# Attention output kept in SBUF, projections moved into the attention, a written order and an f32 tile before the experts

## The chip, the core and the metric

The kernel runs on one core of one Trainium2 chip. The metric is the device time of one execution in microseconds. The core has five engines that run side by side and meet through semaphores: TensorE (PE, matmuls; PEld are its weight loads), VectorE (DVE), ScalarE (ACT), GpSimd (POOL) and SyncE (SP, which here only issues DMAs). Sixteen DMA engines serve the queues that SP and POOL fill.

## The reference

One layer over 1024 tokens of width 1024, all in float32. Cut to what matters:

```python
def reference(x, w_in, ..., w_out, ln1_g, ln1_b, w_route_group, ..., w_gate, w_up, w_down, ln2_g, ln2_b):
    proj = einsum(x, w_in)                     # q, k, v, indexer, z, xbc, dt
    att = dsa_attention(q, k, v, iq, ik, iw)   # 8 heads of 64, each query keeps its 256 best keys
    ssd = ssd_mixer(z, xbc, dt, ...)           # chunked state-space scan, 8 chunks of 128
    mixed = concatenate([att, ssd]) @ w_out
    x = layer_norm(ALPHA * x + mixed, ln1_g, ln1_b)
    # 16 experts in 4 groups: the best group, its 2 best experts
    for e in range(16):
        hid = silu(x @ w_gate[e]) * (x @ w_up[e])          # width 256
        y = y + gates[..., e:e + 1] * (hid @ w_down[e])
    return layer_norm(ALPHA * x + y, ln2_g, ln2_b)
```

## The kernel before

Tokens are worked in eight blocks of 128. Matrices go through PE in float32r, and where precision matters an operand is split into a high part (a copy by ACT, `hi_act`) and a rest (a subtraction by DVE, `lo_dve`), so that one product takes three matmuls. The order of the instructions on each engine is chosen when the program is built, by a planner that simulates the engines and takes the first ready instruction by program order; at run time each engine and each DMA queue executes its list strictly in order. `tc.manual_schedule` makes the order as written binding for the engines that it names; `tc.issue_after` puts an instruction behind another on its engine. Buffers come from pools; a tile of a tag with n buffers waits until the oldest user of its buffer is done.

The stages: input projections, indexer and the choice of keys (0 to about 250 us), the state-space part (to about 370 us), attention over the blocks in `ORDER` = 7, 6, ..., 0 (from about 300 us), the step to the experts, the expert tiles, and the last normalisation.

**Attention and projection.** Python generators emit small steps, and `weave` mixes several of them by weights. `attn(b, nxt)` ends with `to_mix`, which transposes the block's output and writes its two parts (L808 to L810), and stores them to a DRAM tensor `td`. `mix(b)` loads them back (`ai`, L990), with the state-space part (`si`) and the block of x (`xb`), and makes 48 matmuls of 128x512 with the split w_out (`woh`, `wol`, L1006), adds x (L1010), takes the statistics (POOL raises the variance to the power -0.5, L554), transposes for the router (L1019), makes the router's 8 f32 matmuls (L1024; each is two instructions), writes the normalised rows to `hd` and `yd` (L1036, L1037), and, outside the last two blocks, goes on with `route`. `route(b)` ranks the experts, counts with two small matmuls (L1076, L1077), forms the places in the expert lists (`idx`, L1087), and scatters token and gate into `lst` by two indirect DMAs of POOL (L1094). `MIXAT` says with which attention block the projections of which earlier one are woven: before, block number i (in the order) with the projection of i - 2, so that those of the last two blocks, 1 and 0, follow the attention.

**Step to the experts** (L1161 to L1218). `pick` chooses the four fullest experts early (`EE`); `fill_up` declares the first 128 places of the two fullest as full, so that their first tiles can be gathered before the last two blocks are routed. Weights arrive in pieces of 1 MB in five raw buffers `er` (`fetch`, L862 to L865): two for gate and up, one for down, per expert. `split_expert` splits each piece in four (L880) into slots, the first in `eb`, the others in the memory of `woh` and `wol`; a piece whose split is done lets the piece five later be fetched. `expert_tile` gathers 128 rows by the list (`gather`, L888), transposes them (L898), multiplies by gate and up (24 matmuls, L909), applies silu, transposes, multiplies by down (12 matmuls, L934), scales by the gate and adds the rows to `yd` in DRAM by an indirect DMA (L941). The block from L1199 on emits, in written turns, the rest of block 0's `mix` (m0), the routes of blocks 1 and 0 (r1, r0), the two early tiles (t0, t1), the splits of their experts (sp0, sp1) and `order`, which sorts the experts by their counts; the planner is still free in it, since `MAN` is empty. One further tile (`NG0` = 1) is gathered there; its ids are loaded by SP (L1214).

**Expert tiles.** 22 further tiles follow in the order of `PLAN`, each with its gather three tiles ahead (`AHEAD`, L1244), and then `finish`.

Of the kernel before, what the change touches and what calls it, by code (L numbers as in the profile page):

```python
# [12 lines left out]
F32 = mybir.dt.float32  # L13
# [41 lines left out]
MIXAT = {i: (i - 2,) for i in range(2, NB)}  # L55
# [9 lines left out]
NG0 = 1  # L65
HFT = 1
PPT = 'po'
FO = 3
# [38 lines left out]
def f(ap):  # L107
    return ap.bitcast(F32)


def body(ctx, tc, I, out, dbg):
# [80 lines left out]
    td = dram.tile([S, D], F32, name="td")  # L192
# [608 lines left out]
    def attn(b, nxt):  # L801
# [90 lines left out]
    def expert_tile(W, ids, xg, al):  # L892
        th = al([P, KC, P], F32R, "th")
        tl = al([P, KC, P], F32R, "tl")
        for j in range(2):
# [5 lines left out]
            lo_dve(tl[:, js, :], pt, th[:, js, :])  # L901
# [13 lines left out]
        V.tensor_tensor(sg, ag[:, 256:], sg, op=OP.mult)  # L915
        ph2 = psum([P, 2, P], "ph2", "po")
        for k in range(2):
            T.transpose(ph2[:, k, :], sg[:, k * P:(k + 1) * P], ident)  # L918
        hh = al([P, 2, P], F32R, "hh")
        hl = al([P, 2, P], F32R, "hl")  # L920
        hi_act(hh, ph2)
        lo_dve(hl, ph2, hh)
# [3 lines left out]
        hi, lo = W["d"]  # L926
        for hf in range(2):
# [3 lines left out]
            for k in range(2):  # L931
                for j in range(3):
                    l, r = ((hh, hi), (hl, hi), (hh, lo))[j]
                    T.matmul(ad_, l[:, k, :], r[:, k, fs], start=i == 0, stop=i == 5)  # L934
                    i += 1
# [9 lines left out]
    with ExitStack() as ph:  # L945
# [41 lines left out]
        def mix_load(b):  # L987
            ao, so = (wc.tile([P, KC, P], F32R, name=nm, bufs=2) for nm in ("ai", "si"))
            for t, src in ((ao, td), (so, sd)):
                SY.dma_start(f(t), src[b * P:(b + 1) * P, :].rearrange("p (k t) -> p k t", t=P))  # L990
            xb = wc.tile([P, D], F32, name="xb", tag="xb", bufs=4)
            SY.dma_start(xb, x_d[b * P:(b + 1) * P, :])
            return ao, so, xb

        def mix(b, loaded=None):
            while (b, 0) not in done:
                yield
            ao, so, xb = loaded or mix_load(b)
# [37 lines left out]
            SY.dma_start(hd[b * P:(b + 1) * P, :], xb)  # L1036
# [64 lines left out]
        def order():  # L1101
            sq = [P, NE, NE]
            key, w1, cnt, rank = (wc.tile([P, NE], F32, name=nm) for nm in ("key", "w1", "cnt", "rank"))
            cc = wc.tile([P, 2, NE, NE], F32, name="cc", tag="rT", bufs=2)
# [19 lines left out]
            V.tensor_copy(ovi, ov)  # L1124

# [22 lines left out]

# [217 lines left out]
```

## Time and profile before

| | us |
|---|---|
| median of 3 runs | 908.57 (906.67 to 912.49) |
| the profiled execution | 908.86 |
| its span, first to last instruction | 907.2 |

A line of a timeline gives the start in us from the start of the span, the duration in us (for several instructions, from the first start to the last end), the engine, the line of the kernel, the operation, the tiles (written <- read) and the count; in brackets stands how long the engine sat idle before it and what released it. A matmul's duration contains its way through the array, so the distance from start to start tells more than the duration. PEclk is the granted TensorE clock as a share of 2.4 GHz; 0.50 is 1.2 GHz.

### The profile page before, as it was taken

What the parts mean: (1) busy time and instruction counts of PE and PEld (TensorE: products, weight loads), DVE (VectorE), ACT (ScalarE), POOL (GpSimd) and SP (SyncE); (2) the same over time, 40 slices, a digit from 0 to 9 for tenths busy, and PEclk for the clock granted to TensorE, in tenths of its full rate; (3) what the DMA queues carried; (4) which work ended last, traced back from release to release, by engine and by line L of the source; (5) the groups of instructions that cost most, each with busy time, mean ns of one, the idle gap of its engine ahead of it and who ended that gap; (6) DMA issues with size and microseconds to landing.
All of it is one profiled execution on the core that took longest, in us unless ns stands there. A gap on an engine that the chain in (4) does not pass through costs nothing. (4 is left out here: it accounts for less than half of the span.)

```text
span 907.2 us, 12832 instructions
## 1 busy us (share of the span) xinstructions
PE 789.6 (87%) x4084; PEld 649.5 (72%) x4085; DVE 663.2 (73%) x1644; ACT 507.2 (56%) x1074; POOL 222.1 (24%) x203
## 2 busy tenths in 40 slices
PE   6999789999997999899999999987998989969800
PEld 4898568887775678788898877765886767758600
DVE  3678978879576999768866865865775858739348
ACT  3467777882455876655434422634765657638323
POOL 2211000001387373250010111132122223132225
PEclk9999899999997999999999998997999999979955
DMA  8303112311434325873333335978899989989374
GB/s 232 106 24 93 37 69 94 117 47 68 132 128 157 99 70 208 257 266 117 105 105 118 140 117 182 337 247 253 237 278 270 316 260 283 324 255 260 60 225 183
DMA packets 90742, 155.95 MB, mean 172 GB/s; under 512 B 14613, under 2 KB 60837, under 8 KB 90666
## 3 DMA queue, kind: packets, MB, share of 16 engines
q1 hardware_dynamic: 83242, 129.87, 42.7%
q0 software_dynamic: 7424, 25.19, 11.7%
q8 instruction: 33, 0.54, 0.3%
q14 instruction: 43, 0.35, 0.1%
HBM read 109.78 MB, written 45.25 MB: 171 GB/s over the span
## 5 line engine op out<-in xcount | busy, mean ns | idle before, releaser
L232 PE MATMUL acc<-whl,xh 128*128 128x512 f32 (+1 forms) x384 | 121.6, 391 | 2.1 <-ACT whl L124 0.7
L232 PEld LDWEIGHTS acc<-whl,xh 128*128 128x128 f32 x384 | 72.8, 190 | 17.5 <-ACT whl L124 1.4
L909 PE MATMUL ag<-eb,th 128*128 128x512 f32 x224 | 79.9, 423 | 4.7 <-ACT th L124 4.7
L232 PE MATMUL acc<-whl,xl 128*128 128x512 f32 (+1 forms) x192 | 75.9, 396 | 0.0
L124 ACT ACTIVATE ph<-pt 128x512 fp32r<-128x512 f32 (+1 forms) x80 | 43.3, 551 | 56.9 <-PE pt L777 54.0
L941 POOL DMA_INDIRECT yd<-yt,ids x24 | 40.6, 1692 | 138.4 <-DMA yd<-yt,ids 31.9
L253 POOL TENSOR_TENSOR r<-rt,rt 128x448 f32<-128x448 f32 (+1 forms) x16 | 22.8, 1426 | 196.6 <-DVE rt L252 180.0
L360 PE MATMUL acc<-xh,whl 128*128 128x512 f32 x192 | 64.0, 411 | 6.7 <-ACT u L124 6.7
L909 PEld LDWEIGHTS ag<-eb,th 128*128 128x128 f32 x224 | 44.9, 201 | 16.0 <-ACT th L124 6.6
L765 ACT ACTIVATE lt<-lt,mn 128x1024 f32<-128x1024 f32 (+7 forms) x64 | 49.3, 773 | 11.2 <-DVE mn L762 10.9
L127 DVE TENSOR_TENSOR tl<-pt,th 128x512 fp32r<-128x512 f32 x48 | 32.2, 685 | 30.9 <-ACT th L124 30.6
L127 DVE TENSOR_TENSOR plo<-pt,ph 128x512 fp32r<-128x512 f32 (+1 forms) x80 | 49.8, 630 | 6.4 <-ACT ph L124 5.9
L880 DVE TENSOR_TENSOR woh<-er,woh 128x512 fp32r<-128x512 f32 x64 | 41.9, 687 | 13.9 <-ACT woh L124 12.3
L398 ACT ACTIVATE scra<-sc,mid 128x1024 bf16<-128x1024 f32 (+3 forms) x56 | 49.2, 879 | 4.2 <-DVE gef L428 1.7
L360 PEld LDWEIGHTS acc<-xh,whl 128*128 128x128 f32 x192 | 37.8, 199 | 15.4 <-ACT u L124 7.5
L909 PE MATMUL ag<-eb,tl 128*128 128x512 f32 x112 | 48.1, 429 | 0.6 <-DVE tl L127 0.5
L124 ACT ACTIVATE woh<-er 128x512 fp32r<-128x512 f32 x64 | 37.2, 623 | 18.8 <-DMA er<-w_up 11.2
L124 ACT ACTIVATE th<-pt 128x512 fp32r<-128x512 f32 x48 | 27.7, 595 | 34.3 <-PE pt L898 33.9
L124 ACT ACTIVATE eb<-er 128x512 fp32r<-128x512 f32 x64 | 38.8, 630 | 14.2 <-DMA er<-w_up 7.8
L880 DVE TENSOR_TENSOR wol<-er,wol 128x512 fp32r<-128x512 f32 x64 | 41.1, 683 | 6.7 <-ACT wol L124 4.2
L777 PE MATMUL pt<-ident,lt 128*128 128x128 f32 x288 | 44.8, 276 | 1.3 <-ACT lt L765 0.8
L880 DVE TENSOR_TENSOR eb<-er,eb 128x512 fp32r<-128x512 f32 x64 | 41.7, 687 | 5.7 <-ACT eb L124 3.6
(363 smaller groups left out, 2304.9 us busy)
## 6 DMA issues: line engine op xcount, KB each, us to landing
er<-w_gate SPq DMA_DIRECT2D x32, 512.0 KB
er<-w_up SPq DMA_DIRECT2D x32, 512.0 KB
er<-w_down SPq DMA_DIRECT2D x16, 1024.0 KB
xb<-x SPq DMA_DIRECT2D x16, 512.0 KB
raw<-w_in SPq DMA_DIRECT2D x8, 512.0 KB
qd<-qs SPq DMA_DIRECT2D x8, 512.0 KB
sd<-so SPq DMA_DIRECT2D x8, 512.0 KB
qb<-qd SPq DMA_DIRECT2D x8, 512.0 KB
```

Source lines behind the costliest of these rows:

```text
L124: A.activation(hi, src, AF.Copy)
L127: V.tensor_tensor(lo, src, f(hi), op=OP.subtract)
L232: T.matmul(acc[:, :n], l[:, b, k, :], r[:, k % 2, :n], start=i == 0, stop=i == 3 * KC - 1)
L253: G.tensor_tensor(dst, t1, t2, op=OP.add)
L360: T.matmul(acc, w[:, k, :], xx[:, 4 * hf:4 * hf + 4, k, :], start=i == 0, stop=i == 3 * KC - 1)
L398: A.activation(scra[:, :nk], sc[b], AF.Sign, bias=at, scale=-1.0, accum_out=dst)
L765: A.activation(lt[:, :nk], lt[:, :nk], AF.Exp, bias=mn[:, h:h + 1], scale=-1.0, accum_out=rs[:, h:h + 1])
L777: T.transpose(pt[:, c:c + P], L[b, 2 * p + j][:, kt * P:(kt + 1) * P], ident)
L880: e.tensor_tensor(lo[x], raw[x], f(hi[x]), op=OP.subtract)
L909: T.matmul(ag, l[:, k, :], r[:, k % 4, :], start=i == 0, stop=i == 3 * KC - 1)
L941: G.indirect_dma_start(out=yd, out_offset=bass.IndirectOffsetOnAxis(ap=ids[:, 0:1], axis=0), in_=yt, in_offset=None, compute_op=OP.add)
```

## The change

The attention output of all blocks but the first stays in SBUF: `attn` writes it into the `ai` tile that `mix` reads, and `td` shrinks to one block. The projections of two more blocks are emitted with the attention: those of numbers 4 and 5 both at 6, and the matmuls of number 6 (block 1) with the last attention block; only block 0's stays behind it. `fill_up` and the gathers of the two early tiles move ahead of the last attention block. In the step to the experts the written turns are new, and binding for DVE and PE. The second early tile (t1) multiplies the raw f32 weights with unsplit f32 rows, one matmul in the place of three. Three tiles of the plan are gathered in the step (`NG0` = 3), their ids are loaded by POOL, and the scatters of t0 and t1 come behind the gathers on POOL. Block 0's `hd` store is issued by POOL. The gathered tiles alternate between two pools (`al1`, `al2`), in the place of one ring of four.

```diff
-MIXAT = {i: (i - 2,) for i in range(2, NB)}
+MIXAT = {2: (0,), 3: (1,), 4: (2,), 5: (3,), 6: (4, 5)}
-NG0 = 1
+NG0 = 3
...
-        o = wb.tile([P, KC, P], F32R, name="ao", bufs=1)
-        to_mix(done[b, 2], o)
-        SY.dma_start(td[b * P:(b + 1) * P, :].rearrange("p (k t) -> p k t", t=P), f(o))
-        done[b, 0] = True
+        if b == ORDER[0]:
+            o = wb.tile([P, KC, P], F32R, name="ao", bufs=1)
+            to_mix(done[b, 2], o)
+            SY.dma_start(td, f(o).rearrange("p k t -> p (k t)"))
+        else:
+            o = wc.tile([P, KC, P], F32R, name="ai", bufs=2)
+            to_mix(done[b, 2], o)
+        done[b, 0] = o
...
-    def expert_tile(W, ids, xg, al):
+    def expert_tile(W, ids, xg, al, raw=None, fine=False):
+        split = raw is None
+        kind = F32R if split else F32
...
         for k in range(KC):
-            for j in range(3):
-                hi, lo = W[k // 4]
-                l, r = ((th, hi), (tl, hi), (th, lo))[j]
-                T.matmul(ag, l[:, k, :], r[:, k % 4, :], start=i == 0, stop=i == 3 * KC - 1)
+            for l, r in ((th, W[k // 4][0]), (tl, W[k // 4][0]), (th, W[k // 4][1])) if split else ((th, raw[k // 4]),):
+                T.matmul(ag, l[:, k, :], r[:, k % 4, :], start=i == 0, stop=i == (3 * KC if split else KC) - 1)
                 i += 1
-            if k % 4 == 3:
+            if k % (2 if fine else 4) == (1 if fine else 3):
                 yield
...
-            SY.dma_start(hd[b * P:(b + 1) * P, :], xb)
+            (G if b == ORDER[-1] else SY).dma_start(hd[b * P:(b + 1) * P, :], xb)
...
+        def early_gathers():
+            ids = [rp.tile([P, 2], I32, name="ids", bufs=XB + 2) for j in range(2)]
+            for j in range(2):
+                SY.dma_start(ids[j], lst[bass.ds(EE[j] * SL, P), :])
+            return [(x, gather(x, al0)) for x in ids]
...
+            if i == NB - 1:
+                fill_up()
+                first = early_gathers()
+                m1 = mix(ORDER[NB - 2], mix_load(ORDER[NB - 2]))
+                w.append((9, islice(m1, 9)))
             emit(*w)
...
-        last = [(b, mix_load(b)) for b in ORDER[NB - LAG:]]
-        fill_up()
...
-        emit((16, mix(*last[0])), (8, split_expert(pre[0], 0, (0, 1), more=more0)))
...
+        b1, b0 = ORDER[NB - LAG:]
+        m0 = mix(b0, mix_load(b0))
+        for m in range(NR):
             fetch(EE[m // 3], m // 3, m % 3)
+        for _ in islice(m1, 3):
+            pass
+        t0 = expert_tile(pre[0], *first[0], al0, fine=True)
+        t1 = expert_tile(None, *first[1], al0, [raw_of(1, i) for i in range(3)], fine=True)
+        sp0, sp1 = split_expert(pre[0], 0, more=more0), split_expert(pre[1], 1, more=more0)
+
+        def early_ids():
+            ids = [rp.tile([P, 2], I32, name="ids", bufs=XB + 2) for j in range(NG0)]
+            for j in range(NG0):
+                G.dma_start(ids[j], lst[bass.ds(EE[PLAN[j][0]] * SL + PLAN[j][1], P), :])
+            return ids
...
-            go((m0, MM + 2), (r1, 1), (t0, 1), (m0, 1), (r1, 1), (m0, 1), (t0, 1), (m0, 2))
-            r0 = up(route(b0, RL[b0]), HPR)
-            go((r0, 1), (m0, 1), (r0, 1), (t0, 1), (r1, 1), (r0, 1), (t0, 1), (sp0, 4), (t0, 1), (sp1, 4), (t0, 1))
-            go((t1, 2), (sp1, 4), (t1, 1), (sp1, 4), (t1, 1))
...
+            with tc.manual_schedule(engines={mybir.EngineType.DVE, mybir.EngineType.PE}):
+                r1, o_ = route(b1, RL[b1]), order()
+                go((m0, 3), (r1, 2), (sp0, 4), (m0, 1), (r1, 9), (t0, 2), (m0, 2), (sp0, 4), (m0, 2), (t0, 1),
+                   (t1, 2), (t0, 1), (m1, 9), (m0, 2), (t0, 1), (m0, 1), (t0, 1), (m0, 1))
+                r0 = route(b0, RL[b0])
+                go((r0, 2), (t0, 1), (t1, 1), (r0, 9), (t0, 1), (t1, 1), (sp0, 4), (t1, 2), (m0, 9), (t0, 1))
+                ids = early_ids()
+                early_q = [(x, gather(x, al2 if j else al0), PLAN[j][0]) for j, x in enumerate(ids)]
+                go((t1, 1), (sp1, 4), (t1, 2))
+                with tc.issue_after(marks["gather"].ins):
+                    go((t0, 9))
+                go((sp1, 4), (o_, 1), (sp1, 4))
+                with tc.issue_after(marks["gather"].ins):
+                    go((t1, 9))
...
-    wkb = {"xg": XB, "yt": 3}
+    wkb = {"xg": XB // 2, "yt": 3}
...
+    turns = chain.from_iterable([al1] * (XB // 2) + [al2] * (XB // 2) for _ in range(len(PLAN)))
```

In `go((g, n), ...)` each pair takes n steps of a generator. The first six steps of m0 are its 48 matmuls, the seventh adds x for the second half, the eighth takes the statistics, the ninth and tenth transpose, the eleventh is the router, the twelfth forms the router's sums, the last normalises and stores. Of a tile with `fine` the first two steps transpose, the next four multiply by gate and up, then come silu, the second transposes, down, and the scatter.

## Rows read from the trace of the kernel before

**Rows 1.** The page, part 1: busy us, share of span, instructions.
```profile
PE 789.6 (87%) x4084; PEld 649.5 (72%) x4085; DVE 663.2 (73%) x1644; ACT 507.2 (56%) x1074; POOL 222.1 (24%) x203
```
**Rows 2.** Windows: us, busy us (instructions) by engine, then clock, DMA share, GB/s.
```profile
511.00:573.40 62.40, 58.46 (x322) 48.97 (x320) 41.99 (x178) 17.23 (x51) 8.83 (x9) 0.95 0.46 160
573.40:584.70 11.30, 11.27 (x48) 9.08 (x49) 9.64 (x33) 6.73 (x15) 3.27 (x3) 1.00 1.03 365
584.70:602.00 17.30, 16.84 (x97) 14.04 (x95) 13.55 (x46) 9.30 (x17) 4.03 (x3) 1.00 1.03 368
602.00:619.30 17.30, 8.83 (x32) 5.79 (x31) 9.42 (x35) 3.70 (x6) 6.35 (x5) 0.84 0.51 123
619.30:630.40 11.10, 10.36 (x34) 7.92 (x35) 5.65 (x9) 5.69 (x10) 4.31 (x5) 0.64 0.91 252
630.40:857.00 226.60, 209.16 (x969) 166.59 (x967) 157.65 (x268) 140.27 (x268) 52.50 (x37) 0.96 0.89 262
```
**Rows 3.** Timeline of PE around the step to the experts.
```profile
570.95 1.96 PE L1024 MATMUL pr<-gbw,rT 128*128 128x20 f32 x16
573.43 0.74 PE L1006 MATMUL ac<-woh,ai 128*128 128x512 f32 x2 [0.52 <-DMA ai<-td]
...
584.50 0.39 PE L1006 MATMUL ac<-wol,si 128*128 128x512 f32 x1
584.73 0.60 PE L898 MATMUL pt<-ident,xg 128*128 128x128 f32 x4
...
619.29 1.97 PE L898 MATMUL pt<-ident,xg 128*128 128x128 f32 x8 [5.24 <-DMA xg<-hd,ids]
```
**Rows 4.** Timeline of POOL.
```profile
550.16 1.52 POOL L554 TENSOR_TENSOR mv<-mv,nh 128x1 f32<-128x1 f32 x1 [5.67 <-DVE mv L553]
...
604.88 1.44 POOL L1094 DMA_INDIRECT lst<-pay,idx  x1 [0.30 <-issue]
610.94 1.61 POOL L941 DMA_INDIRECT yd<-yt,ids  x1 [4.62 <-ACT hh L124]
612.86 1.01 POOL L888 DMA_INDIRECT xg<-hd,ids  x1 [0.30 <-issue]
```
**Rows 5.** Timeline of SP's DMA queue.
```profile
558.50 0.32 SPq L810 DMA_DIRECT2D td<-ao  x1
559.03 0.41 SPq L865 DMA_DIRECT2D er<-w_gate  x1
...
610.03 0.34 SPq L1214 DMA_DIRECT2D ids<-lst  x1
```
**Rows 6.** Timeline of DVE.
```profile
577.20 0.69 DVE L880 TENSOR_TENSOR woh<-er,woh 128x512 fp32r<-128x512 f32 x1
...
590.01 1.27 DVE L1034 SCALAR_TENSOR_TENSOR xb<-xb,mv,g1r 128x1024 f32<-128x1024 f32 x1
...
594.72 0.21 DVE L1028 TENSOR_SCALAR nm<-mv 128x1 f32<-128x1 f32 x1 [1.04 <-POOL mv L554]
...
602.92 0.16 DVE L1087 CAST idx<-ixf 128x2 int32<-128x2 f32 x1
```
**Rows 7.** The chain that ended last: start, us, what.
```profile
612.86 5.90 DMA xg<-hd,ids
```
**Rows 8.** Timeline of PE, an f32 matmul of 512 columns and its successor.
```profile
342.17 1.02 PE L685 MATMUL pst<-xe,bt 128*128 128x512 f32 x2
343.02 0.38 PE L625 MATMUL pm<-ident,y 128*128 128x128 f32 x2
```
**Rows 9.** Window behind the gap, columns as in rows 2.
```profile
620.00:625.00 5.00, 4.26 (x12) 2.97 (x12) 1.98 (x3) 1.88 (x4) 3.82 (x4) 0.50 0.95 193
```
**Rows 10.** Timeline of PE, two later stalls in the expert tiles.
```profile
743.66 1.94 PE L898 MATMUL pt<-ident,xg 128*128 128x128 f32 x8 [2.56 <-DMA xg<-hd,ids]
...
809.49 1.09 PE L898 MATMUL pt<-ident,xg 128*128 128x128 f32 x4 [7.04 <-DMA xg<-hd,ids]
```
**Rows 11.** Timeline of ACT, the first weights.
```profile
565.22 2.19 ACT L124 ACTIVATE eb<-er 128x512 fp32r<-128x512 f32 x4 [7.01 <-DMA er<-w_up]
```

More of the change, by code (lines that the diff above doesn't have):

```diff
@@ L191, in body @@
     sd = dram.tile([S, D], F32, name="sd")
-    td = dram.tile([S, D], F32, name="td")
+    td = dram.tile([P, D], F32, name="td")
     mk = {i: kvp.tile([P, (i + 1) * P], BF16, name=f"mk{i}") for i in range(2, NB)}
@@ L900, in expert_tile @@
             hi_act(th[:, js, :], pt)
-            lo_dve(tl[:, js, :], pt, th[:, js, :])
+            if split:
+                lo_dve(tl[:, js, :], pt, th[:, js, :])
             yield
@@ L918, in expert_tile @@
             T.transpose(ph2[:, k, :], sg[:, k * P:(k + 1) * P], ident)
-        hh = al([P, 2, P], F32R, "hh")
-        hl = al([P, 2, P], F32R, "hl")
+        hh = al([P, 2, P], kind, "hh")
         hi_act(hh, ph2)
-        lo_dve(hl, ph2, hh)
+        if split:
+            hl = al([P, 2, P], F32R, "hl")
+            lo_dve(hl, ph2, hh)
         yield
@@ L931, in expert_tile @@
             for k in range(2):
-                for j in range(3):
-                    l, r = ((hh, hi), (hl, hi), (hh, lo))[j]
-                    T.matmul(ad_, l[:, k, :], r[:, k, fs], start=i == 0, stop=i == 5)
+                for l, r in ((hh, W["d"][0]), (hl, W["d"][0]), (hh, W["d"][1])) if split else ((hh, raw[2]),):
+                    T.matmul(ad_, l[:, k, :], r[:, k, fs], start=i == 0, stop=i == (5 if split else 1))
                     i += 1
@@ L997, in mix @@
                 yield
-            ao, so, xb = loaded or mix_load(b)
+            so, xb = loaded or mix_load(b)
+            if b == ORDER[0]:
+                ao = wc.tile([P, KC, P], F32R, name="ai", bufs=2)
+                SY.dma_start(f(ao).rearrange("p k t -> p (k t)"), td)
+            else:
+                ao = done[b, 0]
             for hf in range(2):
@@ L1168, in more0 @@
                 fetch(EE[(3 * n + i + NR) // 3], (3 * n + i + NR) // 3, (i + NR) % 3)
-        for m in range(FO):
+        b1, b0 = ORDER[NB - LAG:]
+        m0 = mix(b0, mix_load(b0))
+        for m in range(NR):
             fetch(EE[m // 3], m // 3, m % 3)
-        last = [(b, mix_load(b)) for b in ORDER[NB - LAG:]]
-        fill_up()
         pre = [{}, {}]
-        tags = {"th": ("ai", 2), "tl": ("si", 2), "xg": ("xb", 4), "yt": ("rT", 2)}
-        def al0(shape, dt, name):
-            tag, bufs = tags.get(name, (name, 1))
-            return wc.tile(shape, dt, name=name, tag=tag, bufs=bufs)
-        first = []
-        for j in range(2):
-            ids = rp.tile([P, 2], I32, name="ids", bufs=XB + 2)
-            SY.dma_start(ids, lst[bass.ds(EE[j] * SL, P), :])
-            first.append((ids, gather(ids, al0)))
-        for m in range(FO, NR):
-            fetch(EE[m // 3], m // 3, m % 3)
-        emit((16, mix(*last[0])), (8, split_expert(pre[0], 0, (0, 1), more=more0)))
-        b1, b0 = last[0][0], last[1][0]
-        m0 = up(mix(*last[1]), HPM)
-        t0, t1 = (expert_tile(pre[j], *first[j], al0) for j in range(2))
-        sp0, sp1 = split_expert(pre[0], 0, ("d",), more=more0), split_expert(pre[1], 1, more=more0)
+        for _ in islice(m1, 3):
[8 more added lines that the diff above has]
+            return ids
         def go(*gs):
@@ L1197, in go @@
                     next(g, None)
[L1199 to L1217 removed]
+        if True:
+            with tc.manual_schedule(engines={mybir.EngineType.DVE, mybir.EngineType.PE}):
[12 more added lines that the diff above has]
+                    go((t1, 9))
             marks.clear()
     wk = pool("workD", stack=es, side="right")
[L1221 removed]
+    wkb = {"xg": XB // 2, "yt": 3}
     def al1(shape, dt, name):
@@ L1244, in ids_for @@
         SY.dma_start(ids, lst[bass.ds(rank(r) * SL + t0, P), :])
-        return ids, gather(ids, al1), r
+        return ids, gather(ids, next(turns)), r
     turn, last = [], {}
```

41 lines of the change are left out of this document (16 added, 25 removed).

## The prediction, made before the changed kernel ran

> **What bounds the kernel now.** I read four views, in this order. The page's busy times first [rows 1]: TensorE (PE) is busy for 87% of the span, so only its idle time and its low clock can be won; the change adds no parallel resource. Then the windows [rows 2], to find where that idle time lies. PE works through most of the attention, through block 0's projection (573.4 to 584.7) and the first expert work (584.7 to 602), and then does 8.83 us of work in 17.3 us (602 to 619.3), followed by 11.1 us at a mean clock of 0.64. That hole is the step to the experts. Third, PE's timeline [rows 3] says what ends the hole: a gather of token rows, for which PE sat 5.24 us. Fourth, the queues in front of that gather [rows 4 to 6]: the last block's projection ends at 584.73; its expert index is there at 603.1; the two list scatters end at 606.32; the ids are loaded at 610.03, the gather is issued at 612.86 and lands 5.9 us later [rows 7]. This chain of 34.6 us, from the end of the last projection to the first transposes of the queue-driven tiles at 619.29, is the limit; PE's own work under it (two early tiles, the router's small matmuls) fills only part of it. Later, in the 226.6 us of expert tiles, PE is 92% busy with DMA at 0.89 [rows 2]: both are near their limit there, and 17.4 us of PE idle are left in a few stalls.
>
> **Part 1: the attention output stays in SBUF, and two projections move into the last attention blocks.** Seven of the eight round trips through td go (1 MB each, with two SP issues). DMA is at 0.46 in that stretch [rows 2], so the bytes are worth nothing; one wait is: PE's 0.52 us at 573.43 [rows 3], inside the idle sum below. The work of block 2's projection moves from the attention of block 0 to that of block 1, and block 1's from behind the attention into that of block 0. PE does the same work; what can be won is what it loses between 511.02 and 573.43: 62.40 - 58.46 = 3.9 us of idle and (1 - 0.95) x 62.4 = 3.1 us of low clock [rows 2], 7.0 us in all. Not all of it goes. Today block 1's matmuls cover the time in which block 0's output is copied and split after its transposes; now they are used up before that, and about 1.0 to 1.7 us open up (a copy and a subtraction of 512 columns, the latter at 0.69 us [rows 6]). I take 5.0 of the 7.0, with bounds of 0 and 7.0. Block 0's projection then starts at 568.4. It is 48 matmuls in 11.30 us, 0.235 us each [rows 3]; the written order puts eight transposes of the first early tile (0.9 us: half of the 1.97 us that they take at half clock [rows 3]) and block 1's rank matmuls (0.4 us) inside it, so it ends at T0 = 568.4 + 11.3 + 1.3 = 581.0, against 584.73.
>
> **Part 2: the written order of PE and VectorE (DVE), from T0 on.** Before, the index came 18.4 us after T0: block 0's sum waited among weight splits (0.69 us each), and GpSimd's power waited behind a scatter, so that the next step ran only at 594.72 [rows 6]. In the written order DVE has behind the sum the statistics (two passes over 512 columns at about 0.69 us and two small ones, 1.8 us), then the power on GpSimd (1.52 us and its hand-over [rows 4]) under block 1's normalisation (2 x 1.27 us [rows 6]): done by T0 + 6. PE reaches the router's matmuls after 24 matmuls (5.6) and 16 transposes (1.8); they take 1.9 us [rows 3] and end at T0 + 9.3, and so set the pace. From there to the index today's 8.4 us (594.72 to 603.08 [rows 6]) contain a normalisation, a split, a product and a wait for PE; without them I take 4.0, an estimate: T0 + 13.3. The payload stands behind it now (0.7 us), and the two scatters follow as before (3.2 us): T0 + 17.2. Then 3.7 us to the issue of the ids and 2.8 us to the gather [rows 4, 5], plus 0.5 us for the two other ids issued ahead of it: T0 + 24.2. The first early tile's yd scatter, which today takes 1.61 us of GpSimd just ahead of the gather [rows 4], is put behind all three gathers, so nothing is to be added for it.
>
> Beside this runs block 0's normalised row store hd, now on GpSimd's queue, which the gather needs too. DVE normalises after four splits (2.7 us) and one small operation: T0 + 14.0 + 2.7 + 0.4 + 2.6 = T0 + 19.7. The trace has no plain store from GpSimd. From below it is bounded by the ids load (2.8 us from issue to the gather's start [rows 4, 5]), from above by the gather of equal size (5.9 us [rows 7]): it lands at T0 + 22.5 to T0 + 25.6, so it costs the gather between 0 and 1.4 us. The gather's row is nearest in size and queue, but reads single rows; I take 0.3. The gather is issued at T0 + 24.5, lands at T0 + 30.4, and PE starts 0.5 us later, at T0 + 30.9 = 611.9. Against 619.29 that is 7.4 us earlier.
>
> Here a rule of the Trainium skill speaks against the change. GpSimd's indirect DMAs occupy it for 1.0 to 1.6 us each where SP's issues take 0.3 us [rows 4, 5]. "DMA: Bandwidth & Descriptors", section "SWDGE vs HWDGE vs iDMA", says that a plain transfer belongs on SP's or ScalarE's queue and only accumulating, casting or irregular ones on GpSimd's; its latency table puts the first byte at about 1 us against 0.6 us. By those figures, an estimate, store and ids would cost 0.4 us each in this chain, and the sum would be 0.8 us higher. No trace here has the same transfer on both queues.
>
> **Part 3: the f32 early tile.** An f32 matmul of 512 columns is two instructions and 0.85 us (342.17 to 343.02 [rows 8]). The second early tile has 12 of them, 10.2 us, for 36 of 0.235 us, 8.5 us: 1.7 us more PE, while DVE loses two splits of 0.69 us and a shorter one, and the tile no longer waits for the 12 splits of its expert. This lies beside the chain: from T0 on PE has 24 matmuls (5.6), 16 transposes (1.8), the router (1.9), the f32 tile (10.2), the first tile's 12 (2.8) and small ones (1.0): 23.3 us for 30.9. So its price is nothing while the 7.6 us of slack stay positive, and up to 1.7 us otherwise. The slack has a price of its own: the clock, 0.50 at 620 to 625 after today's idle [rows 9], will again be low when the tiles start; I count no gain for it.
>
> What is late next is DVE: its splits for expert 1 and the ordering of the experts move behind the gather's issue. Today it is busy for 9.42 us between 602 and 619.3 [rows 2]; eight splits more make 15 us, from T0 + 18 on. The tile's own split is wanted at T0 + 33.8 (2.7 us after PE's transposes begin, as today, when its first matmul came at 622.0). It just fits; 0 to 2 us, and I take 0.
>
> **Part 4: the rest.** Three weight pieces are fetched later, because the f32 tile holds the raw buffers; they are wanted only two tiles on, about 19 us after PE's start, and land in some 9 us. Three gathers instead of one go early; today PE had no long wait for the second or third. Zero for both. From PE's start on the same 22 tiles remain, 237 us with their stalls today; I carry them over.
>
> **Sum.** The profiled execution took 908.86 us (span 907.2 and 1.66 outside), 0.3 above the median of 908.57. 908.86 - 7.4 = 901.5. I predict **901**; the bounds of the terms (0 to 7.0 us of Part 1, 0 to 1.4 of the store, 0 to 2 of DVE) alone give 899 to 910.
>
> **The rivals.**
> (a) Denser than I think. If the attention loses nothing (2 us more), and PE waits less than 2 us for the gather (about 5.6 us more) and so starts the tiles at full clock (of today's 11.1 x 0.36 = 4.0 us, 2 to 4), the time is 890 to 892; with one of the three, 895 to 899. For it: weights may be fetched before the attention ends, since today their first issue stands right behind the td store that goes [rows 5]. Against it: the end of the chain, 12.4 us from the scatters to the gather's landing [rows 4, 5, 7], is not shortened by the change.
> (b) Given back. The tiles start 7 us earlier, but three weight pieces and the closed loop of buffers, scatters and gathers make one more stall like those of 743.66 and 809.49 (2.6 to 7.0 us, plus low clock around it [rows 10]). Time 905 to 911. For it: DMA is at 0.89 over the whole stage. Against it: 0.51 between 602 and 619.3, with fetches held by buffers, not by the DMA engines [rows 2].
> (c) The written order turns against the kernel. DVE executes the four or eight splits of expert 0 ahead of block 0's sum, wherever the weights are; today they land 6.2 us after their issue at 559.03 [rows 5, 11], and the written order allows about 9 us after the projection's start before the sum moves. Ids loads of the early gathers now stand on SP's queue ahead of the fetches. Each us beyond is one at the end: weights that land 16 us after the projection's start take the whole gain, 20 us give 912, 28 us give 920. For it: nothing can pass a waiting instruction in a written order. Against it: the weights' buffers come free no later than today.
> (d) The order does not do what it says: GpSimd, SP and ScalarE are still ordered by the planner, and if it puts the ids' wait ahead of the hd store, the store lands 3 to 5 us later: 904 to 906.
>
> **How the numbers follow.** A measurement of this kernel tells about 1% from no change (three runs of before spread over 6 us), so the line is at 899.5. Forecast, 897 to 905: 0.44, of which 0.16 beyond the line. (a) 890 to 899, 0.30, beyond it. (b) 0.09 and (d) 0.07, within. (c) 0.10, of which 0.08 slower by more than 1%. Faster 0.46, same 0.46, slower 0.08. The range leaves out the lowest tail of (a) and most of (c): 889 to 911.
>
> **What would show it.** Right: block 0's projection ends near 581; the index 13 us behind it; three gathers in a row on GpSimd with the yd scatters behind; PE's first queue-driven transposes near 612, idle 5 to 8 us before; f32 matmuls at 0.85 us. Wrong: DVE waiting for ScalarE's copy of weights ahead of the sum; GpSimd waiting for the hd store; more idle than 17.4 us in the expert tiles.

## The result, and the profile after

The changed kernel takes 918.44 us (median of 9 runs, 916.5 to 930.0), the kernel before beside it on the same chip 911.27 (9 runs): a ratio of 1.0101, 95% interval 1.0069 to 1.0133. It is slower by about 1%, where 901 was forecast, with 889 to 911 as the range. The profiled execution took 917.38 us with a span of 915.7, against 907.2 before, so 8.5 us are to be found. Most runs of one kernel lie within some 4 us of their median, so a sum is read from ratios and a place from profiles.

Windows of the changed kernel, cut at its own landmarks (columns as in [rows 2]):
```profile
514.18:577.50 63.32, 58.26 (x326) 49.73 (x324) 37.72 (x174) 13.47 (x43) 10.54 (x11) 0.95 0.31 105
577.50:592.00 14.50, 14.24 (x61) 11.35 (x62) 9.39 (x36) 11.00 (x23) 2.25 (x2) 0.88 0.99 340
592.00:622.00 30.00, 23.70 (x101) 15.33 (x99) 24.34 (x67) 12.65 (x23) 9.11 (x11) 1.00 0.65 200
622.00:626.00 4.00, 2.64 (x9) 1.86 (x9) 3.79 (x12) 1.19 (x2) 1.35 (x1) 0.50 1.08 385
```
The first line is the stretch of the last two attention blocks with the projections woven in: 63.32 us with 58.26 of work and a clock of 0.95, against 62.40, 58.46 and 0.95 [rows 2]. Nothing of its idle time was won. It also begins 3.2 us late (514.18 against 511.02). The step behind block 0's projection did get shorter, 30.0 us with 23.70 of work in it.

PE's timeline of the changed kernel, at the places of [rows 3]:
```profile
570.67 1.01 PE L791 MATMUL pn<-ii,o 128*128 128x64 f32 x4 [3.15 <-DVE xb L1019]
...
577.50 0.70 PE L1015 MATMUL ac<-woh,ai 128*128 128x512 f32 x1 [0.69 <-ACT ai L123]
...
591.72 0.40 PE L1015 MATMUL ac<-wol,si 128*128 128x512 f32 x1
...
622.09 1.97 PE L903 MATMUL pt<-ident,xg 128*128 128x128 f32 x8 [5.14 <-DMA xg<-hd,ids]
...
626.77 0.80 PE L913 MATMUL ag<-eb,tl 128*128 128x512 f32 x1 [2.03 <-DVE tl L126]
```
T0 is the end of block 0's projection, taken as the start of the instruction behind its last matmul (584.73 before, 591.95 here), and R the start of the first transposes of the queue tiles. The 8.5 us split like this:

| stretch | before | forecast | after | forecast change | change |
|---|---|---|---|---|---|
| block 0's projection starts | 573.43 | 568.4 | 577.50 | -5.0 | +4.1 |
| it lasts, to T0 | 11.3 | 12.6 | 14.5 | +1.3 | +3.2 |
| T0 to R | 34.6 | 30.9 | 30.1 | -3.7 | -4.4 |
| R to the span's end | 287.9 | 287.9 | 293.6 | 0 | +5.7 |

So the third line, with most of the working, came out as a sum; the first, second and fourth did not. Against the forecast, a span of 907.2 - 7.4 = 899.8, the kernel is 15.9 us long: R stands at 622.09 where 611.9 was forecast (10.2), and 5.7 come behind it.

What PE waited for at 570.67 is on VectorE, and what VectorE waited for is on SyncE's queue. Both timelines of the changed kernel (the queue as in [rows 5]), and GpSimd's for the scatter in front of them:
```profile
569.93 1.29 DVE L1019 SCALAR_TENSOR_TENSOR xb<-xb,ac 128x512 f32<-128x512 f32 x2 [7.77 <-DMA xb<-x]
```
```profile
388.33 0.43 SPq L1005 DMA_DIRECT2D ai<-td  x1
...
550.33 0.43 SPq L1046 DMA_DIRECT2D yd<-xb  x1
565.48 0.91 SPq L1168 DMA_DIRECT2D ids<-lst  x2
566.50 0.83 SPq L996 DMA_DIRECT2D xb<-x  x2
567.53 0.39 SPq L868 DMA_DIRECT2D er<-w_gate  x1
```
```profile
563.35 0.96 POOL L1103 DMA_INDIRECT lst<-pay,idx  x1 [0.31 <-issue]
```
The queue issues nothing between 550.8 and 565.48. At its head stand the two list loads of the early gathers, which wait for block 2's list scatters; behind them stand block 1's x and all expert weights. VectorE reaches the add of that x to block 1's projection, sits 7.77 us, and keeps attention block 0's steps behind it waiting. The row at 388.33 is a second late load: `ai` of the first block, issued near 375 in the kernel before.

GpSimd's timeline, at the step ([rows 4] before) and at the end of the expert tiles:
```profile
606.23 0.96 POOL L1103 DMA_INDIRECT lst<-pay,idx  x1 [0.30 <-issue]
608.63 1.76 POOL L1214 DMA_DIRECT2D ids<-lst  x3 [1.45 <-DMA lst<-pay,idx]
610.38 0.54 POOL L1045 DMA_DIRECT2D hd<-xb  x1
617.70 1.01 POOL L891 DMA_INDIRECT xg<-hd,ids  x1 [6.77 <-PE ad L939]
...
850.76 1.56 POOL L946 DMA_INDIRECT yd<-yt,ids  x1 [6.24 <-DMA yd<-yt,ids]
857.49 1.55 POOL L946 DMA_INDIRECT yd<-yt,ids  x1 [5.16 <-DVE sg L919]
864.42 1.55 POOL L946 DMA_INDIRECT yd<-yt,ids  x1 [5.39 <-ACT yt L942]
871.37 1.55 POOL L946 DMA_INDIRECT yd<-yt,ids  x1 [5.39 <-DMA yd<-yt,ids]
```
The last rows are the scatter-adds of tile outputs. They follow each other 6.7 to 7.0 us apart. Some of the named releasers had long been done; the last is for an output that ScalarE finished at 864.2, so it waited 7 us for the one before it. In the kernel before the last one left at 864.88, so the end is 6.5 us later although PE's last tile is only some 3 us later. The first scatter-adds of a queue tile and the last of all, in the kernel before and then in the changed one:
```profile
641.08 1.61 POOL L941 DMA_INDIRECT yd<-yt,ids  x1 [16.12 <-ACT yt L937]
...
864.88 1.55 POOL L941 DMA_INDIRECT yd<-yt,ids  x1 [5.36 <-DMA yd<-yt,ids]
```
```profile
649.14 1.96 POOL L946 DMA_INDIRECT yd<-yt,ids  x1 [11.80 <-DVE woh L883]
```
From the first queue tile's scatter-add to the last it is 223.8 us before and 222.2 here.

### The profile page after: what moved, and what is told of

Its sections match the earlier page's. It is cut to its first block, busy times and chain, and to the rows that moved or that the text cites. A ratio compares the mean times of both kernels' runs of the same rounds, so it can differ in the third digit from the quotient of the medians.

```text
span 915.7 us, 12770 instructions
## 1 busy us (share of the span) xinstructions
PE 792.2 (87%) x4072; PEld 648.4 (71%) x4073; DVE 661.9 (72%) x1641; ACT 506.0 (55%) x1074; POOL 229.3 (25%) x207
## 5 line engine op out<-in xcount | busy, mean ns | idle before, releaser
L946 POOL DMA_INDIRECT yd<-yt,ids x24 | 42.3, 1761 | 127.0 <-DMA yd<-yt,ids 45.0
L913 PEld LDWEIGHTS ag<-eb,th 128*128 128x128 f32 x224 | 44.5, 199 | 10.3 <-ACT th L123 1.0
L1015 PE MATMUL ac<-woh,ai 128*128 128x512 f32 x128 | 44.4, 427 | 1.4 <-ACT ai L123 0.7
L783 PE MATMUL po<-ph,vhl 128*128 128x256 f32 x144 | 42.3, 309 | 2.2 <-ACT ph L123 1.3
```

Of the source, the lines that this page charges most:

```text
L783: T.matmul(po, vhl[:, kt, :], x[:, i * 256:i * 256 + 256], start=kt == 0 and x is ph_, stop=kt == b and x is pl_)
L946: G.indirect_dma_start(out=yd, out_offset=bass.IndirectOffsetOnAxis(ap=ids[:, 0:1], axis=0), in_=yt, in_offset=None, compute_op=OP.add)
L1015: T.matmul(ac, src[:, o + k % 4, :], w[:, k, fs], start=i == 0, stop=i == 3 * KC - 1)
```

## The experiments

Each experiment was measured beside the kernel before. Ratios are to that kernel; the changed kernel's is 1.0101, and a gain or loss against it is the difference of the two ratios times 911.27. A ratio is known to 0.002 to 0.004, so the difference of two ratios is known to about 4 us: a gain of 4 us is only just clear of nothing, and there the profiles have to say what happened.

**The list loads on SyncE's queue.** Two ways of taking them from ahead of block 1's x:
```diff
-                first = early_gathers()
                 m1 = mix(ORDER[NB - 2], mix_load(ORDER[NB - 2]))
+                first = early_gathers()
```


> The two list loads of the early gathers stand behind block 1's load of x on SyncE's queue instead of ahead of it; nothing else is moved. Theory 1 (the queue): in the changed kernel the add of x to block 1's projection waited 7.77 us on VectorE at 569.93 for a load that was issued only at 566.5, behind the list loads at 565.5; so the wait goes, block 0's projection starts 4 to 8 us ahead of 577.5, and the time falls by 4 to 7 us from the changed kernel's 918. Rival (the weaving itself): VectorE and TensorE have too little room beside the last two attention blocks, the wait only moves to the next operation, and the time stays within 2 us.


```diff
-                SY.dma_start(ids[j], lst[bass.ds(EE[j] * SL, P), :])
+                G.dma_start(ids[j], lst[bass.ds(EE[j] * SL, P), :])
             return [(x, gather(x, al0)) for x in ids]
```


> The two list loads are issued by GpSimd, so that SyncE's queue has no wait on the list scatters at all. Theory 1: as with the x load moved ahead, 4 to 7 us less than 918, and the first fetches of expert weights leave at about 551 instead of 567.5, which may give another 1 to 2 us if they were late for the first splits. Rival: GpSimd now stands in its queue until the list is written (it was at 563) and small GpSimd steps of attention block 0 come later; then it is 0 to 3 us worse than the run with the x load ahead.

Measured: 1.0058 (1.003 to 1.0086), 3.9 us less than the changed kernel (0.0043 x 911.27), with the x load ahead, and 1.0036 (1.0012 to 1.0059), 5.9 us less, with the list loads on GpSimd. In both, block 0's projection starts at 572 to 573 instead of 577.5. The first falls short of its range, because the step grew: T0 to R is 34.0 us there and 30.3 in the second. ScalarE's timeline of the first says why:
```profile
577.26 2.20 ACT L123 ACTIVATE eb<-er 128x512 fp32r<-128x512 f32 x4 [1.40 <-DMA er<-w_up]
581.56 2.19 ACT L123 ACTIVATE eb<-er 128x512 fp32r<-128x512 f32 x4 [2.10 <-DMA er<-w_up]
```
The weights still stood behind the list loads, and the written order has the splits of expert 0 ahead of block 0's sum. With the queue free (SyncE's timeline of the second) x and the first weights leave at once:
```profile
551.05 3.85 SPq L996 DMA_DIRECT2D xb<-x  x2
555.17 0.40 SPq L868 DMA_DIRECT2D er<-w_gate  x1
```
VectorE's wait of 7.77 us for x is gone in both runs. The queue theory holds, by these places and by the time of the second; the time of the first alone would not show it. Neither rival does.

**The late load of the first block's attention output.**
```diff
-            so, xb = loaded or mix_load(b)
             if b == ORDER[0]:
-                ao = wc.tile([P, KC, P], F32R, name="ai", bufs=2)
+                ao = wc.tile([P, KC, P], F32R, name="ai0", tag="rT", bufs=2)
                 SY.dma_start(f(ao).rearrange("p k t -> p (k t)"), td)
             else:
                 ao = done[b, 0]
+            so, xb = loaded or mix_load(b)
```


> The attention output of the first block, the one that still goes through DRAM, is loaded into a tile of another ring and ahead of the other loads of its projection, so that the load is issued at about 375 as in the kernel before instead of 388.3. Theory 2: the 3.2 us by which the changed kernel is late after the first projection (394.7 against 389.3 for its first matmul, 514.2 against 511.0 for block 1's start) come from this load; 2.5 to 3.5 us less than 918. Rival: the attention work that took its place on TensorE was due anyway and what is gained at 395 is given back before 514; under 1 us.

Measured: 1.0034 (1.0012 to 1.0056), 6.1 us less than the changed kernel, about twice what was expected. SyncE and PE in this run:
```profile
375.13 0.33 SPq L1004 DMA_DIRECT2D ai<-td  x1
```
```profile
388.89 0.70 PE L1015 MATMUL ac<-woh,ai 128*128 128x512 f32 x2
```
and PE in the changed kernel:
```profile
394.75 1.20 PE L1015 MATMUL ac<-woh,ai 128*128 128x512 f32 x2
```
There that first matmul ran at 394.75, and it and the next few at half speed. 5.9 us are gained there, and the gain is whole 180 us later: block 0's projection starts at 571.9 and R comes at 616.5, both 5.6 earlier than in the changed kernel. I had measured the loss at 511, after the changed kernel had made up part of it with work taken ahead; that was too late in the trace. VectorE's wait for x is still there, 7.62 us, so the two waits are separate. The edit changes two things, the buffer (no longer from the ring that the later blocks' outputs share) and the place of the load in the program. No run here separates them, so which of the two had held the load is not shown.

**The low part that PE waited for at 626.77.** The last four splits of expert 1 go behind the first queue tile's own (shown without the lines that hold their subtractions behind the tile's own split):
```diff
-                go((sp1, 4), (o_, 1), (sp1, 4))
+                go((sp1, 4), (o_, 1))
 ...
+            if i == 0:
+                go((t_, 2), (sp1, 9))
```


> The last four low parts of expert 1's down weights stand behind the two low parts of the first queue tile in VectorE's order. Theory 3: the 2.03 us that TensorE waited at 626.77 for the low part go, and the clock comes back that much sooner: 2 to 3 us less than 918. Rival: the scatter-adds into the result, each of which waits for the one before (6.9 us apart at the end), set the end, and what is gained at 626 shows only if the first of them starts earlier: 0 to 1 us.

Measured: 1.015 (1.0115 to 1.0185), 4.5 us more. PE of this run:
```profile
629.74 0.79 PE L913 MATMUL ag<-eb,tl 128*128 128x512 f32 x1 [0.16 <-DVE tl L126]
...
656.04 0.79 PE L913 MATMUL ag<-eb,th 128*128 128x512 f32 x1 [6.97 <-ACT th L123]
```
ScalarE, with a split of fetched weights:
```profile
653.05 2.19 ACT L123 ACTIVATE wol<-er 128x512 fp32r<-128x512 f32 x4 [12.12 <-DMA er<-w_up]
```
and SyncE:
```profile
624.55 0.34 SPq L1265 DMA_DIRECT2D ids<-lst  x1
644.64 0.36 SPq L179 DMA_DIRECT2D g2r<-ln_g  x1
645.19 0.43 SPq L179 DMA_DIRECT2D b2r<-ln_b  x1
645.90 0.39 SPq L868 DMA_DIRECT2D er<-w_gate  x1
```
The wait of 2.03 us went (0.16 is left), and 6.97 us came 26 us later for weights that ScalarE got at 653.05 and whose fetch left at 645.90, since SyncE's queue now stood for 20 us. At its head stood two loads for the last normalisation (L179), and behind them the fetches; the step that splits the last piece also emits the next fetch, so the edit moves that fetch in the program too. R to the end is 298.6 us in this profile, 5.0 longer. Neither theory had this: with the splits moved, SyncE's queue came out in another order, and that cost more than the move gave.

**The chain of scatter-adds.**
```diff
+    y2 = dram.tile([S + P, D], F32, name="y2")
+    ys = chain.from_iterable([yd, y2] for _ in range(len(PLAN) + 8))
-        G.indirect_dma_start(out=yd, out_offset=...
+        G.indirect_dma_start(out=next(ys), out_offset=...
+            SY.dma_start(y2.rearrange("(b p) d -> p b d", p=P), zf[:, None, :].to_broadcast([P, NB + 1, D]))
```


> The expert tiles add their rows in turn into two tensors instead of one, so that a scatter-add waits for the last but one and not for the one before it. The second tensor isn't read, so half of the experts' part is left out of the output; one more 4.7 MB store of zeros goes ahead of the attention. Theory 4 (the chain of scatter-adds sets the end): in the changed kernel the last four stand 6.7 to 7.0 us apart and the last is issued at 871.4 for a tile whose output was ready at 864.2; then it is issued within 1 us of its tile, gathers no longer stand behind waiting scatters on GpSimd, and the time is 6 to 12 us less than 918. Rival (TensorE sets the end): under 3 us.

Measured: 0.9842 (0.9803 to 0.988), 23.6 us less than the changed kernel. GpSimd of this run:
```profile
841.06 1.89 POOL L948 DMA_INDIRECT y<-yt,ids  x1 [11.07 <-ACT hh L123]
847.53 1.55 POOL L948 DMA_INDIRECT yd<-yt,ids  x1 [4.58 <-ACT hh L123]
851.65 1.55 POOL L948 DMA_INDIRECT y<-yt,ids  x1 [2.57 <-ACT yt L944]
```
Each now leaves when its tile is done. R to the end is 274.9 us against 293.6. Of these 18.7, the 21 links between the first queue tile's scatter-add and the last account for 14.3 (222.2 us to 207.9), 3.2 come from the end, where nothing waits for the tensor that isn't read, and 1.3 from the first scatter-add. A further 4.2 us stand ahead of R, where the store of zeros had SyncE's queue ordered differently; they have nothing to do with the chain. Theory 4 holds, and by more than it said. The other runs agree with it. In ten profiles (before, changed, and all but the two with fewer waits, the one with the early `order`, and the one with all edits) the stretch from the first queue tile's scatter-add to the last takes 221.8 to 224.4 us, while from R to the last it is anything from 245.6 to 255.0: the chain keeps its length and begins later.

The same with the whole output: tiles of one expert never share a row of the data, so the second of a pair needs no wait.
```diff
+        if W is not None and sc and sc[-1][0] is W:
+            tc.declare_no_dep(st_.ins, sc[-1][1].ins, reason="an expert's list has each row once")
+        elif len(sc) > 1 and sc[-2][0] is sc[-1][0]:
+            tc.add_manual_dep(st_.ins, sc[-2][1].ins.name, both, reason="both tiles of the expert before")
+        sc.append((W, st_))
```


> Of the changed kernel only one thing is different: where two tiles of the same expert follow each other (6 of the 24 scatter-adds), the second scatter-add doesn't wait for the first, since a list holds each row of the data once; the next one waits for both. The output stays whole. Theory 4 (the chain of scatter-adds paces the expert tiles): the run with two result tensors lost 18.7 us between the first transposes of the queue tiles and the end (293.6 to 274.9) by halving the chain; 6 of 24 waits less should give about half of that or less, 4 to 9 us. Rival: the last five scatter-adds, of experts with one tile each, still wait for one another and set the end as before: under 2 us.

Measured: 0.9964 (0.9941 to 0.9987), 12.5 us less than the changed kernel. The profiled execution took longer than all others of this kernel (913.4 us); in it R to the end is 287.3 us, 6.3 less than in the changed kernel, of which 6.1 lie in the 21 links (216.1 us). So between 6 and 12 us come from leaving out six waits of 24: by the profile within what was expected, by the ratio above it, and known to about 4 us.

**The row store that the gather waits for.**
```diff
-            (G if b == ORDER[-1] else SY).dma_start(hd[b * P:(b + 1) * P, :], xb)
+            SY.dma_start(hd[b * P:(b + 1) * P, :], xb)
```


> Block 0's row store goes back to SyncE's queue; only the lists stay on GpSimd's. Theory 5: the gather waited for this store, which left GpSimd at 610.4 and let the gather go at 617.7; SyncE issues the other store of the same rows at 610.1, so the store leaves at about the same time, and if a GpSimd store of 512 KB takes longer to land than a SyncE one, the first transposes of the queue tiles come 1 to 3 us earlier than 622.1 and the time falls by as much. Rival: the landing takes as long from either queue and the time is the same within 0.5 us.

Measured: 1.0094 (1.0062 to 1.0126), no different from the changed kernel. The DMA view of 600 to 625 us (size and us from issue to landing) has one line for this store in either kernel; changed, then this run:
```profile
hd<-xb POOLq DMA_DIRECT2D x1, 512.0 KB, 6.5
```
```profile
hd<-xb SPq DMA_DIRECT2D x1, 512.0 KB, 5.1
```
From issue to the gather's start it is 7.3 us and 6.0 us. The gather left 24.1 us after T0 instead of 25.7, but took 5.6 us to PE's start instead of 4.4, so T0 to R is only 0.4 us shorter: the shorter landing is as the theory said, the unchanged time as the rival said. The Trainium skill, "DMA: Bandwidth & Descriptors", section "SWDGE vs HWDGE vs iDMA", gives SyncE's queue the faster setup; the sign agrees here, and 1.3 us is more than the 0.4 us that I had worked out from its latencies.

**Adding up.** First the two edits that pay, then the normalising steps ahead of four splits, `(m0, 9), (sp0, 4)` for `(sp0, 4), ..., (m0, 9)` in the written order, then the row store on SyncE as well:

> The two edits that gave time by themselves, together: the lists of the early gathers loaded by GpSimd, and the first block's attention output loaded early into a tile of its own. If the two waits are independent, the gains add: 4.2 us and 5.6 us at the first transposes of the queue tiles, which then stand at about 612 (before 619.3, changed 622.1), and the time is 904 to 909, faster than the kernel before. Rival: with block 7's projection earlier the list scatters of block 2 come earlier too, so the first edit had less left to give; then 909 to 913.

> As the run before it, and the two normalising steps of block 0 stand ahead of the last four low parts of expert 0's down weights (2.5 us) on VectorE. Theory 5 again: the store of those rows is what the gather waits for, so the gather, and all behind it, comes 2.0 to 2.5 us earlier. Rival: the down product of the first early tile waits for the low parts, and its scatter-add, which heads the chain of scatter-adds, comes as much later: no gain at the end.

> As the run with the normalising steps moved ahead, and block 0's row store on SyncE's queue. There the store stood on GpSimd behind the list loads, which wait for the list scatters, and left at 601.3, no earlier after the projection's end (18.2 us) than without the move (18.3); on SyncE it leaves at about 14 us after the end. Theory 5b: the gather then waits for the lists and not for the store, and the first transposes of the queue tiles come 27 to 28 us after the projection's end instead of 30.1; 2 to 3 us less than 906.5. Rival: the lists land no earlier than the rows and the step stays at 29.5 to 30.1 us.

Measured: 0.9964 (0.9938 to 0.999) at 906.45 us for the first. Its landmarks add up as expected:
```profile
566.53 0.50 PE L1015 MATMUL ac<-woh,ai 128*128 128x512 f32 x1 [0.69 <-ACT ai L123]
...
611.42 1.97 PE L903 MATMUL pt<-ident,xg 128*128 128x128 f32 x8 [5.29 <-DMA xg<-hd,ids]
```
The second has the same 0.9964 (0.9939 to 0.9988): no gain, and not by the rival's reason. Its GpSimd timeline:
```profile
599.59 1.77 POOL L1214 DMA_DIRECT2D ids<-lst  x3 [1.42 <-DMA lst<-pay,idx]
601.34 0.54 POOL L1045 DMA_DIRECT2D hd<-xb  x1
607.92 1.17 POOL L891 DMA_INDIRECT xg<-hd,ids  x1 [6.04 <-DMA hd<-xb]
```
The rows were ready 2.4 us sooner, but the store stands behind the list loads in GpSimd's queue and left 18.4 us after T0, as in the changed kernel. Here rival (d) of the prediction cost something, 2.7 us between the rows' end at 598.63 and 601.34; in the changed kernel, with the same order, the rows were ready at 610.06 and next to nothing was lost (0.3 us). With the store on SyncE, T0 to R falls to 25.7 us, and the time is 1.0006 (0.9982 to 1.003), not better but by the medians 3.8 us worse than without it. PE and ScalarE of that run:
```profile
607.85 1.09 PE L903 MATMUL pt<-ident,xg 128*128 128x128 f32 x8 [0.70 <-DMA xg<-hd,ids]
613.21 0.79 PE L913 MATMUL ag<-eb,th 128*128 128x512 f32 x1 [4.27 <-ACT th L123]
616.74 0.80 PE L913 MATMUL ag<-eb,tl 128*128 128x512 f32 x1 [2.74 <-DVE tl L126]
```
```profile
612.56 1.08 ACT L123 ACTIVATE th<-pt 128x512 fp32r<-128x512 f32 x2 [4.68 <-DVE w L1125]
```
The gather came 5 us earlier and PE then waited 7 us: ScalarE's high part for a step of the expert ranking, `order`, on VectorE (its releaser there is `w`, L1125), and VectorE's low part for four splits behind that ranking. The first queue scatter-add left at 639.4, against 638.7 without the edit.

> All edits together: lists of the early gathers on GpSimd's queue, the early load of the first block's attention output, the normalising steps ahead, block 0's row store on SyncE, and no wait between the scatter-adds of two tiles of one expert. By the sums of the single runs 895 to 902, faster than the kernel before by 1 to 1.6 per cent. Rival: once the chain of scatter-adds is shorter, TensorE and the weight splits set the pace and the edits ahead of the experts no longer add to it: 900 to 905.

> As the run with all edits together, and the ranking of the experts stands on VectorE ahead of the splits of expert 1 instead of between the second and the third of them, and the first queue tile takes its eight products with low parts of the rows last. In the run with the row store on SyncE the first transposes came 25.5 us after the projection's end, as expected, but the first product stood 4.27 us for ScalarE's high part, which waited for a step of the ranking on VectorE, and then 2.74 us for VectorE's low part. Theory 6: these two waits are where the earlier gather was given back; both go, and the time is 2 to 6 us less than the 897.5 of the run with all edits. Rival: the chain of scatter-adds, still 18 links long, has the end again, and the time is within 1.5 us of 897.5.

All edits with the pairs: 897.48 us (median of 6 runs), 0.9869 (0.983 to 0.9908), the fastest whole kernel of the study, 1.3% faster than the kernel before and 2.3% (1.0101 to 0.9869) faster than the changed one. The last, with `(o_, 1)` ahead of expert 1's splits and the low products last, is 902.79 us, 0.9919 (0.9893 to 0.9945): slower than the run before it, though only just clear of the spread, and outside both expectations. PE:
```profile
608.46 4.01 PE L915 MATMUL ag<-eb,th 128*128 128x512 f32 x16 [0.30 <-ACT th L123]
615.57 2.08 PE L915 MATMUL ag<-eb,tl 128*128 128x512 f32 x4 [3.10 <-DVE tl L126]
...
701.00 0.80 PE L915 MATMUL ag<-eb,th 128*128 128x512 f32 x1 [5.80 <-ACT th L123]
```
The ranking did hold the high part (4.27 to 0.30), but all three groups of splits still stood ahead of the low part, and those splits, now later, give the raw buffers back later; I take the 5.80 us at 701, for a split of fetched weights, to be that, as in the run with the late splits, and have not tested it. The first queue scatter-add left at 631.2 there, 8.2 us earlier than at 639.4, yet the 21 links took 227.7 us though six waits were left out: something other than the chain paced this run, and what it was is open.

## Why the prediction was wrong

**Part 1, the woven projections** (5.0 us taken, bounds 0 to 7.0; measured 4.1 lost). This step failed, in the placing and not in the amount. The list loads were seen and named in rival (c), but as something ahead of the fetches only; that block 1's x stands behind them too, that VectorE would wait for it in the middle of the attention, and that the lists depend on block 2's scatter at 563, was not followed. I put Part 1's gain at PE's idle time and asked which bytes went, not which load is behind which wait. VectorE waited 7.77 us there, and taking the wait away gave 5.9 us of time. The other half is the first block's `ai` load, the one round trip that stays, for which the sum has no term; it cost 5.6 us at the projection's start and 6.1 us of time. Without both, block 0's projection starts at 566.5, 6.9 us ahead of the kernel before: the weaving is worth what was lost there, my upper bound, and I took 5.0. The projection with what the written order puts into it took 14.5 us for 12.6, at a clock of 0.88, and 14.6 in the run without the waits; this term was 2 us too small, since I had it at full clock. In the run without the waits the two errors cancel: it ends the projection at 581.1, and the forecast was 581.0. Its R is 611.42, against 611.9, so all that it still lacks against the forecast lies behind R.

**Part 2, the step** (30.9; measured 30.1). Right as a sum, by luck in its parts. The index came 12.2 us after T0 (forecast 13.3), and the list loads started 1.44 us after the scatters' end where I had carried over 3.7. The 3.7 us were not SyncE's doing: its list loads of the changed kernel started 1.17 us after the end of their scatter (564.31 to 565.48), and in the kernel before the scatters took 5.1 us from issue to landing, against 2.1 here. The row store left 18.4 us after T0 (forecast 19.7) but needed 7.3 us to the gather's start, above my upper bound of 5.9: a read of the same size was no bound for a store from GpSimd. I had taken 0.3 us for what the store costs the gather, with 1.4 at most; this term failed. In the two runs with the normalising steps ahead, the gather left 25.0 us after T0 with the store on GpSimd and 20.7 with it on SyncE, so there the store held it for some 4 us; here it left after 25.7 where 24.5 was forecast. GpSimd did wait for that store, as the text said would show the step wrong. What cancelled it is that the gather then took 4.4 us to PE's start, where I had carried over 6.4: 18.4 + 7.3 + 4.4 = 30.1 against 19.7 + 4.8 + 6.4 = 30.9.

**Part 3, the f32 tile** (12 matmuls of 0.85 us, hidden). Right: 24 instructions in 10.9 us (1.88 + 5.32 + 3.70), done at 617.0, 5 us before PE's first transposes of the queue tiles. It is at its limit, though: where the gather came 5 us earlier, PE idled only 0.70 behind it.

**VectorE's low part** (0 taken, bounds 0 to 2). Mis-sized at its bound: 2.03 us.

**The expert tiles** (carried over, 0; measured +5.7). This is the second failed step, and it began with an incomplete reading in the first paragraph: that PE and DMA are both near their limit there. A third thing paced them, the scatter-adds into one tensor. The 21 links take 222 to 224 us, 10.6 us each, whenever the whole chain is there, and 207.9 with half of the waits gone; PE is then busy for 94% of the stretch, where it had been 89%. So the end is tied to the moment of the first queue scatter-add, not to R, and that moment is 8.1 us later than before while R is 2.8 later. The 5.7 us are 5.3 more from R to the first queue scatter-add (21.8 us before, 27.1 after), 1.6 less in the links, and 2.0 more behind the last one (42.3 and 44.3), for which no run shows a cause. Of the 5.3 us, 2.0 are the low part; for the rest the timelines show a longer stretch of low clock (0.57 from 622.1 to 634) and PE taking 24 products of the second queue tile ahead of the first one's down product, and neither was tested. Rival (b) had the 905 to 911 of such a loss but placed it in one more stall; the gather stalls of the tiles sum to 10.2 us after and 10.5 before, and PE's idle time there did not grow (17.4 us before, 16.4 after), so the sign that I had named for a loss in the tiles did not show, and the loss was there all the same.

Slower by over 1% had 0.08, all on rival (c), whose mechanism (a written order that waits for late weights) was found in one experiment alone, the one with x moved ahead of the lists. The measured 1.0101 (1.0069 to 1.0133) lies on that line, and the loss had other causes, so it does not speak for that rival.

## What to carry to other kernels

Before an instruction that waits is put into an in-order queue, list what stands behind it there and who waits for that, to the end of the list: here two 1 KB list loads held back a load of x, through it VectorE, and through that the attention. When a stage is busy on every engine, look also for a chain of dependent transfers through one tensor; its pace times its length may be the stage, and then neither an earlier start nor a faster engine shows at the end. A step made shorter is worth what is next in line behind it allows: the gather made 5 us earlier gave nothing, while the ranking and the splits stood behind it unmoved.

## What the runs showed of the hardware

In the changed kernel a scatter-add of 128 rows of 4 KB into DRAM took 6.1 us from issue to landing at the end, where little else moved (850 to 880), and 8.7 to 10.3 us while weights were fetched. As the kernel has the next one into the same tensor wait for it, they followed each other 6.7 to 7.0 us apart at the end and 11 to 12 us apart earlier (786.83, 798.36, 810.26, 821.34); there GpSimd's gathers stood between them too. A plain store of 512 KB took 6.5 us to land from GpSimd's queue and 5.1 from SyncE's, and in the pair of runs with the normalising steps ahead 5.7 and 2.9; other traffic was not the same, so the sign is shown and the size is not. A tiny list load that waited for a scatter started 1.44 us after the scatter's end on GpSimd's own queue and 1.17 us after it on SyncE's, no difference to speak of; the 3.7 us between scatter and list load in the kernel before are a slower scatter (5.1 us to land, against 2.1).
